# Two layers of a hybrid decoder on one core: how the squares of the norms are summed, and what the first norm's squares wait for

## The chip, the core and the metric

The kernel runs on one core of a Trainium2 chip. The metric is the device time of one execution in microseconds (us), as the median of several runs. Engines are named as the profile names them: PE (matrix multiply; PEld is its weight load), DVE (vector engine), ACT (scalar engine), POOL (GpSimd), SP (the queue that issues every DMA of this kernel).

## The reference, cut to what matters

The input is one sequence of 256 tokens with 1024 channels, in float32, and two layers are applied to it. Each layer does this:

```python
xn = rms(x, norm_mix_g)          # x * rsqrt(mean(x*x) + 1e-6) * g
z  = xn @ w_in                   # 7756 columns: mLSTM, sparse attention, differential attention, gates
...                              # three mixers give y_a, y_b, y_c, 512 channels each
x  = x + (sum_b sigmoid(gate_b) * (y_b @ w_branch[b])) @ w_out
xn = rms(x, norm_ffn_g)
g, u = split(xn @ w_gate_up)     # 2 x 2816 columns
x  = x + (silu(g) * u) @ w_down
```

So there are four RMS norms in all: each needs, for every token, the sum of the squares of its 1024 channels.

## The kernel before, in words

**Data.** x is held transposed in SBUF: eight tiles `x[0]` to `x[7]` of 128 channels by 256 tokens (T = 256). The weights come from HBM in chunks of 128 x 1024 floats (512 KB, `chunk`, line 509): a DMA into `raw` (3 buffers), then `split` (line 524): ACT copies it to `whi` in a rounded 32-bit format and DVE subtracts to get the rest, `wlo` (3 buffers each). Each product is three matmuls (`feat`, line 528): whi times the high part of x, whi times its low part, wlo times the high part. The high and low parts of x times the norm's gain are `xg` (`fx` in the norm before the feed-forward), made by `gained` (line 547).

**The norm** (`norm`, line 551) doesn't scale x before the matmuls. It makes the gained parts, and beside them the factor of each token, which is multiplied in when results leave PSUM. The factor: the squares of the eight x tiles are summed into one tile `nacc` of 128 x 256. Two PE transposes bring it to token-major form in PSUM, a DVE reduce over 128 columns gives the sum for each token (`rcol`), DVE and POOL make the reciprocal root, DVE spreads it (`rc`), four PE transposes bring it back, and ACT copies it to `rB`. In the first norm of the program (`first`) two ACT instructions of 1024 columns make the squares (`sq8`) and three DVE additions of 1024, 512 and 256 columns fold them. In the other three norms ACT squares `x[0]` straight into `nacc`, squares the others one by one into `nsq`, and POOL adds each of these seven to `nacc`.

**The opening.** x comes in four DMAs and the first two chunks in halves; `first_pair` (line 630) multiplies them in the order in which they land. The squares of the first norm are recorded with `S.after(w_first[1][1])`: they come after all writes to the low part of the second chunk. The chunks from the third on go through `chunk` in the loop over the pairs of output blocks (`fp`, line 778). Results of a pair leave PSUM through `pad`, a DVE multiplication by `rB`, and a chain of DVE operations (`cv`) follows.

**The order of work.** Nothing is issued as it is written. Each call is recorded with an index; `S.early(n)` lowers the index by n. `schedule` (line 206) then simulates the five engines with a duration for each operation (`cost`, line 354): on each engine it takes the recorded operation that could start first, by index among equals, and holds operations until a buffer of their tag is free. The engines run the resulting lists strictly in order. `S.gang()` makes the matmuls inside it one uninterrupted block. Temporary tiles of tag `w` share 15 buffers (`tmp`, line 473). `PLACED` (line 416) lists the tags whose tiles are laid out first in SBUF, with gaps in bytes.

Of the kernel before, what the change touches and what calls it, by code (L numbers as in the profile page):

```python
# [11 lines left out]
F32 = mybir.dt.float32  # L12
F32R = mybir.dt.float32r
BF16 = mybir.dt.bfloat16
AF = mybir.ActivationFunctionType
OP = mybir.AluOpType
AX = mybir.AxisListType.X
# [376 lines left out]
T = 256  # L394
# [18 lines left out]
BR = (1, 2, 0)  # L413


PLACED = ("whi", "wlo", "nacc", 192, "xg", "y", "h", 192, "w", 224, "mqk", 192, "K1", 416)


def plan():
# [37 lines left out]
def kernel(ctx: ExitStack, tc: tile.TileContext, xT: bass.AP, wts: bass.AP, cst: bass.AP,  # L457
# [6 lines left out]
    S = Order(tc, sbuf, psum)  # L464
    V, A, G, PE, SP = (S.engine(n) for n in ("vector", "scalar", "gpsimd", "tensor", "sync"))
# [4 lines left out]
    def atps(shape):  # L470
        return S.tile(shape, F32, tag="at", name="at", bufs=4, psum=True)

    def tmp(shape, name="w"):
        return S.tile(shape, F32, tag="w", name=name, bufs=NW)
# [6 lines left out]
    K1 = S.tile([128, 256], F32, name="K1")  # L481
# [3 lines left out]
    xs = S.tile([128, 128 + 8 * T], F32, name="x")  # L485
    x = [xs[:, 8 + k * T:8 + (k + 1) * T] for k in range(8)]
    ident, ones = K1[:, 0:128], K1[:, 128:256]
# [19 lines left out]
    widx = [0]  # L507

    def chunk(li):
        i = widx[0]  # L510
        widx[0] += 1
        w = WIDTH[i]
        raw = S.tile([128, CH], F32, tag="raw", name="raw", bufs=3)
        hi = S.tile([128, CH], F32R, tag="whi", name="whi", bufs=3)
        lo = S.tile([128, CH], F32R, tag="wlo", name="wlo", bufs=3)
        src = wts[li, OFFS[i]:OFFS[i + 1]].rearrange("(p c) -> p c", p=128)
        with S.early(600):
            if li == 0 and i < 2:
                return raw, hi, lo, src
            SP.dma_start(raw[:, :w], src)  # L520
            split(raw, hi, lo, 0, w)
        return hi, lo
# [28 lines left out]
    def norm(gcol, wide, xg=None):  # L551

        first = xg is not None
        xg = xg or []
        acc = S.tile([128, T], F32, tag="nacc", name="nacc")
        for k in range(8 - len(xg)):
            g = gcol[:, k:k + 1]
            if not wide:
                a = S.tile([128, 2, T], F32R, tag="xg", name="xg", bufs=8)
            else:  # L560
                if k % 4 == 0:
                    y4 = S.tile([128, 4, 2, T], F32R, tag="y", name="fx", bufs=3)
                a = y4[:, k % 4]
            gained(a, k, g)
            xg.append(a)
        if first:
            sq = S.tile([128, 8 * T], F32, tag="y", name="sq8", bufs=3)
            with S.after(w_first[1][1]):
                for a in (0, 4 * T):
                    A.activation(sq[:, a:a + 4 * T], xs[:, 8 + a:8 + a + 4 * T], AF.Square)  # L570
            for n in (4 * T, 2 * T):
                V.tensor_add(sq[:, 0:n], sq[:, 0:n], sq[:, n:2 * n])
            V.tensor_add(acc, sq[:, 0:T], sq[:, T:2 * T])
        else:
            for k in range(8):
                if k == 0:
                    A.activation(acc, x[k], AF.Square)
                else:
                    sq = tmp([128, T], "nsq")
                    A.activation(sq, x[k], AF.Square)  # L580
                    G.tensor_add(acc, acc, sq)
        ps = atps([128, 2, 128])
        with S.gang():
            for t in range(2):
                PE.transpose(ps[:, t, :], acc[:, t * 128:(t + 1) * 128], ident)
        rcol = S.tile([128, 2], F32, tag="rcol", name="rcol", bufs=2)
        V.tensor_reduce(rcol, ps, axis=AX, op=OP.add)
        V.tensor_scalar(rcol, rcol, 1.0 / D, EPS, op0=OP.mult, op1=OP.add)
        rsqrt_cols(rcol, 2)
        rr = tmp([128, 2, 128], "rc")  # L590
        V.tensor_copy(rr, rcol[:, :, None].to_broadcast([128, 2, 128]))
        ps = atps([128, 2, T])
        with S.gang():
            for i in range(2):
                for t in range(2):
                    PE.transpose(ps[:, i, t * 128:(t + 1) * 128], rr[:, t, :], ident)
        rB = S.tile([128, T], F32, tag="rB", name="rB", bufs=2)
        A.activation(rB, ps[:, 0, :], AF.Copy)
        return xg, rcol, rB


    xg0, w_first = [], [chunk(0), chunk(0)]
    with S.early(10 ** 6):
# [21 lines left out]
        w_first = [w[1:3] for w in w_first]  # L625
# [4 lines left out]
    def first_pair(ps):  # L630
        with S.early(10 ** 6), S.chained():
            keep_warm(WARM)
            seen = [0, 0]

            def passes(j, ks):

                for p, q in ((0, 0), (0, 1), (1, 0)):
                    for k in ks:
                        seen[j] += 1
                        PE.matmul(ps[:, j, :], w_first[j][p][:, k * 128:k * 128 + 128], xg0[k][:, q, :],  # L640
                                  start=sum(seen) == 1, stop=sum(seen) == 48)

            for j, ks in ((0, (0, 1)), (0, (2, 3)), (1, (0, 1, 2, 3)), (0, (4, 5)), (1, (4, 5)),
                          (0, (6,)), (1, (6,)), (0, (7,)), (1, (7,))):
                passes(j, ks)
# [113 lines left out]
                                       op0=OP.mult, op1=OP.subtract)  # L759

    for li in range(L):
        widx[0] = 2 if li == 0 else 0
        c = col[li]
        r = row[li] = S.tile([128, R_N], F32, tag="row", name="row")
        ps_first = mmps([128, 2, T]) if li == 0 else None
        if li == 0:
            first_pair(ps_first)
        xg, rcol, rB = norm(c[:, C_NM:C_NM + 8], False, xg0 if li == 0 else None)
        if li:
            SP.dma_start(r, rows[li:li + 1, :].to_broadcast([128, R_N]))  # L770
# [6 lines left out]
        mqk = []  # L777
        for fp in range(4):
            if li == 0 and fp == 0:
                ps = ps_first  # L780
            else:
                ps = mmps([128, 2, T])
                for j in range(2):
                    w = chunk(li)
                    for k in range(8):
                        feat(ps[:, j, :], w, k * 128, xg[k], k == 0, k == 7)
            qk = S.tile([128, 2, T], F32, tag="mqk", name="mqk", bufs=4)
            for j in range(2):
                f = 2 * fp + j
                pad = pads[j]  # L790
                with S.early(400):
                    V.tensor_mul(pad[:, 3:3 + T], ps[:, j, :], rB)
                v = tmp([128, T], "cv")
                cw = c[:, C_CW + 4 * f:C_CW + 4 * f + 4]
                A.activation(v, pad[:, 0:T], AF.Identity, scale=cw[:, 0:1], bias=c[:, C_CB + f:C_CB + f + 1])
                for m in range(1, 4):
                    V.scalar_tensor_tensor(v, pad[:, m:m + T], cw[:, m:m + 1], v, op0=OP.mult, op1=OP.add)
                A.activation(qk[:, j, :], v, AF.Silu)
            mqk.append(qk)
            if li == 0 and fp == 2:  # L800
                with S.after(w[1]):
                    SP.dma_start(K2, cst[:, 256:1024])
                    SP.dma_start(col[1], cols[1])
            if li == 0 and fp == 3:
                with S.after(w[1]):
                    SP.dma_start(r, rows[li:li + 1, :].to_broadcast([128, R_N]))
                hb, dg, rope = setup(li)


        ps = [mmps([128, 256]) for _ in range(2)]  # L810
        for a in range(2):
            w = chunk(li)
            for t in range(2):
                for kk in range(4):
                    k = 4 * a + kk
# [6 lines left out]
        for t in range(2):  # L822
            j = tmp([128, 256], "junk")
# [19 lines left out]
        for ks in ((0, 1, 2), (3, 4, 5), (6, 7)):  # L843
            w = chunk(li)
# [28 lines left out]
        for t in range(2):  # L873
            nk = 128 * (t + 1)
            m = mask1[:, 128:256] if t == 0 else mask1
            acc = tmp([128, 256], "isc")[:, :nk]
            ps = [atps([128, 2, nk]) for _ in range(2)]
# [5 lines left out]
            for j in range(2):  # L883
                p = ps[j]
                rl = tmp([128, 2, nk], "rl")
                A.activation(rl, p, AF.Relu)
                for hp in range(2):
                    h = 2 * hp + j
# [23 lines left out]
        p = proj512()  # L912
# [5 lines left out]
        w = chunk(li)  # L918
        p = [mmps([128, 512]) for _ in range(2)]
# [4 lines left out]
        w = chunk(li)  # L924
        sv = []
        for t in range(2):
            p = mmps([128, 512])
# [5 lines left out]
        y = [S.tile([128, 4, 2, T], F32R, tag="y", name=f"y{b}", bufs=3) for b in range(3)]  # L933
        for t in range(2):
            yp = atps([128, 4, 128])
            n = 4 // (t + 1)
            for a in range(t + 1):
# [13 lines left out]
                with S.gang():  # L951
                    for i in range(n):
                        for kt in range(t + 1):
                            for j in range(2):
                                h = 2 * n * a + 2 * i + j
# [5 lines left out]
        p = tmp([128, 2, 64], "lamp")  # L961
# [11 lines left out]
        for j, dst in ((2, dqT), (3, dkT)):  # L973
            p = proj512()
# [4 lines left out]
        p = proj512()  # L979
        dv = [evac(p[t], rcol[:, t:t + 1]) for t in range(2)]  # L980
        for t in range(2):
            n = 4 // (t + 1)
# [4 lines left out]
            for hh in range(0, 4, n):  # L987
# [9 lines left out]
                a = tmp([128, nh, nk], "da")  # L997
# [4 lines left out]
                with S.gang():  # L1002
                    for i in range(nh):
                        h = hh + i
# [4 lines left out]
            j = tmp([128, 4, 128], "dj")  # L1009
# [34 lines left out]
        with S.gang():  # L1044
            for t in range(2):
                p = atps([128, 4, 128])
# [21 lines left out]
        for t in range(2):  # L1068
            p = mB[t]
# [11 lines left out]
        for b, (si, ti) in enumerate(((0, 0), (1, 1), (0, 1))):  # L1081
            p = atps([128, 4, 128])
# [7 lines left out]
        p = proj512()  # L1090
# [7 lines left out]
        p = proj512()  # L1098
        mo = [evac(p[t], rh[:, t:t + 1], AF.Tanh).rearrange("p (h d) -> p h d", h=4) for t in range(2)]
        for t in range(2):  # L1100
# [9 lines left out]
            for a in range(2):  # L1110
                V.tensor_copy(den[:, 2 * a:2 * a + 2], nd[a][:, :, 128])
                for i in range(2):
                    j = tmp([128, 128], "mj")
# [25 lines left out]
        for gp in range(12):  # L1139
            ps = mmps([128, 2, T])  # L1140
            for j in range(2):
                w = chunk(li)
# [13 lines left out]
        for n, b in enumerate(BR):  # L1156
            for ep in range(4):
                w = chunk(li)
# [125 lines left out]
```

## Time and profile before

| | |
|---|---|
| median of 3 runs | 909.11 us |
| the three runs | 909.11, 903.57, 916.03 us |
| the profiled execution | 910.13 us |
| its span, first to last instruction | 908.0 us |
| granted PE clock over the span | 1.00 |
| busy: PE, PEld, DVE, ACT, POOL | 897.8, 857.3, 675.6, 536.0, 111.6 us |
| HBM read | 158.27 MB, 175 GB/s over the span |

A line of the timeline gives the start from the beginning of the span, the duration, the engine, the operation with out<-in tiles and shapes, the count, and in brackets the idle time of the engine before it with what ended it. A line of the chain of waits gives start, duration, and the engine and tile that the program's end depended on then. Nearly all instructions carry line 323, from which the planner issues them, so work is told apart by tiles. 2.1 us of the profiled execution lie outside the span.

### The profile page before, as it was taken

The page shows a single profiled execution, that of the slowest core. Times are in us where ns is not written, and L with a number is a line of the kernel's source. Part 1 is how long each engine was busy: PE and PEld are TensorE (multiplying, and loading weights), DVE is VectorE, ACT ScalarE, POOL GpSimd, SP SyncE. Part 2 cuts the span into 40 slices and gives each one's busy share as a digit, 9 for nine tenths or more (in the row PEclk, how much of TensorE's full clock was granted, in tenths as well). Part 3 has the DMA queues.
Part 4 walks back from the last instruction along what each step waited for, and adds up shares of the span by engine and source line. Part 5 has one row for each costly group of instructions (what it writes and reads, how often), then busy time and mean ns, then how long its engine had stood idle before and what let it go on. Part 6 is the DMA issues. An engine that isn't in the chain of part 4 may idle for free.

```text
span 908.0 us, 18059 instructions
## 1 busy us (share of the span) xinstructions
PE 897.8 (99%) x7162; PEld 857.3 (94%) x7162; DVE 675.6 (74%) x1276; ACT 536.0 (59%) x928; POOL 111.6 (12%) x142
## 2 busy tenths in 40 slices
PE   9999999999999999999999999999999999999998
PEld 8978779999999999999999787899999999999998
DVE  6999989766896666665578899897669866666553
ACT  6786677765465444444457857687654655545442
POOL 0333342300021000000110221312000300000000
PEclk9999999999999999999999999999999999999999
DMA  8665524356555555555665554433555555555663
GB/s 260 197 200 183 165 91 126 123 176 196 196 187 186 187 186 187 186 176 189 190 188 181 181 186 141 138 110 125 186 190 194 198 185 191 197 195 189 197 210 102
DMA packets 46453, 160.50 MB, mean 177 GB/s; under 512 B 5408, under 2 KB 6560, under 8 KB 46368
## 3 DMA queue, kind: packets, MB, share of 16 engines
q1 hardware_dynamic: 46368, 159.34, 53.8%
q8 instruction: 56, 0.92, 0.4%
q14 instruction: 29, 0.24, 0.1%
HBM read 158.27 MB, written 1.05 MB: 175 GB/s over the span
## 4 chain that ended last, share of the span: by engine, by line
PE 88%; DVE 6%; POOL 2%; DMA 2%; issue 1%; ACT 1%; ACTq 0%; DVEq 0%
PE mm L323 83%; PE at L323 5%; DVE e L323 2%; DVE wlo L323 2%; POOL s L323 2%; DMA raw<-in_wts_dram 1%; ACT whi L323 1%; DMA x<-in_xT_dram 0%; DVE zr L323 0%; DVE cv L323 0%; DVE y L323 0%; DVE s L323 0%; DVE rot L323 0%; DVE pad L323 0%; DVE xg L323 0%
## 5 line engine op out<-in xcount | busy, mean ns | idle before, releaser
L323 ACT ACTIVATE whi<-raw 128x1024 fp32r<-128x1024 f32 (+3 forms) x304 | 316.5, 1042 | 316.6 <-PE mm L323 150.3
L323 DVE TENSOR_TENSOR wlo<-raw,whi 128x1024 fp32r<-128x1024 f32 (+3 forms) x304 | 364.5, 1200 | 170.8 <-ACT whi L323 169.0
L323 PE MATMUL mm<-fx,whi 128*128 128x256 f32 x1408 | 245.1, 279 | 0.0
L323 PEld LDWEIGHTS mm<-fx,whi 128*128 128x128 f32 x1408 | 214.7, 189 | 0.0
L323 PE MATMUL mm<-fx,wlo 128*128 128x256 f32 x704 | 195.9, 279 | 0.0
L323 PE MATMUL mm<-xg,whi 128*128 128x256 f32 x1024 | 181.4, 280 | 0.3 <-ACT whi L323 0.3
L323 PEld LDWEIGHTS mm<-xg,whi 128*128 128x128 f32 x1024 | 155.4, 188 | 1.7 <-issue 0.7
L323 PE MATMUL mm<-whi,xg 128*128 128x512 f32 (+2 forms) x512 | 149.1, 372 | 1.1 <-DVE pad L323 1.1
L323 PE MATMUL mm<-xg,wlo 128*128 128x256 f32 x512 | 142.5, 281 | 0.8 <-DVE wlo L323 0.8
L323 PEld LDWEIGHTS mm<-fx,wlo 128*128 128x128 f32 x704 | 132.0, 188 | 0.0
L323 PE MATMUL mm<-h,whi 128*128 128x256 f32 x704 | 122.1, 279 | 0.0
L323 PEld LDWEIGHTS mm<-whi,xg 128*128 128x128 f32 x512 | 92.0, 188 | 17.3 <-issue 1.5
L323 PEld LDWEIGHTS mm<-h,whi 128*128 128x128 f32 x704 | 107.4, 189 | 0.0
L323 PE MATMUL mm<-h,wlo 128*128 128x256 f32 x352 | 98.1, 279 | 0.0
L323 PEld LDWEIGHTS mm<-xg,wlo 128*128 128x128 f32 x512 | 95.8, 188 | 1.1 <-DVE wlo L323 1.1
L323 PE MATMUL mm<-wlo,xg 128*128 128x512 f32 (+2 forms) x256 | 94.9, 371 | 0.0
L323 PEld LDWEIGHTS mm<-h,wlo 128*128 128x128 f32 x352 | 66.1, 188 | 0.0
L323 PE MATMUL mm<-y,whi 128*128 128x256 f32 x384 | 65.4, 276 | 0.0
L323 POOL TENSOR_TENSOR nacc<-nacc,nsq 128x256 f32<-128x256 f32 x21 | 20.2, 962 | 348.0 <-ACT nsq L323 210.1
L323 PEld LDWEIGHTS mm<-y,whi 128*128 128x128 f32 x384 | 57.8, 188 | 0.0
L323 PEld LDWEIGHTS mm<-wlo,xg 128*128 128x128 f32 x256 | 48.1, 188 | 7.3
L323 PE MATMUL mm<-y,wlo 128*128 128x256 f32 x192 | 53.0, 276 | 0.0
(199 smaller groups left out, 1083.6 us busy)
## 6 DMA issues: line engine op xcount, KB each, us to landing
raw<-in_wts_dram SPq DMA_DIRECT2D x278, 512.0 KB, 3.4
raw<-in_wts_dram SPq DMA_DIRECT2D x16, 384.0 KB, 3.8
raw<-in_wts_dram SPq DMA_DIRECT2D x4, 498.0 KB, 4.0
raw<-in_wts_dram SPq DMA_DIRECT2D x4, 256.0 KB, 4.8
out_dram<-x SPq DMA_DIRECT2D x8, 128.0 KB, 3.4
row<-in_rows_dram SPq DMA_DIRECT2D x2, 388.0 KB, 5.3
x<-in_xT_dram SPq DMA_DIRECT2D x3, 256.0 KB, 5.0
raw<-in_wts_dram SPq DMA_DIRECT2D x2, 332.0 KB, 3.0
```

The source lines that it names most:

```text
L323: getattr(getattr(nc, o.eng), o.fn)(*args, **kw)
```

## The change

- In `norm`, the accumulator becomes a temporary of tag `w` with two parts of 256 columns, and `nacc` is no longer a tile of its own (1 KB in each partition, taken out of `PLACED`).
- In the three later norms the square of `x[7]` goes from ACT into the second part; POOL adds six squares, not seven. Four transposes instead of two, and the reduce goes over 256 columns for each token.
- In the first norm the two halves of the squares wait for the high parts of the third and the fourth chunk, one each. DVE folds them with two additions (1024 and 512 columns); the last fold is left to the reduce.
- The calls of `chunk` for the third and fourth chunk are recorded right after `first_pair`, before the norm, and used in the loop.

```diff
-PLACED = ("whi", "wlo", "nacc", 192, "xg", "y", "h", 192, "w", 224, "mqk", 192, "K1", 416)
+PLACED = ("whi", "wlo", 192, "xg", "y", "h", 192, "w", 224, "mqk", 192, "K1", 416)
...
-        acc = S.tile([128, T], F32, tag="nacc", name="nacc")
+        acc = tmp([128, 2, T], "nacc")
...
-            with S.after(w_first[1][1]):
-                for a in (0, 4 * T):
-                    A.activation(sq[:, a:a + 4 * T], xs[:, 8 + a:8 + a + 4 * T], AF.Square)
-            for n in (4 * T, 2 * T):
-                V.tensor_add(sq[:, 0:n], sq[:, 0:n], sq[:, n:2 * n])
-            V.tensor_add(acc, sq[:, 0:T], sq[:, T:2 * T])
+            for a in range(2):
+                with S.after(w_next[a][0]):
+                    A.activation(sq[:, 4 * a * T:4 * (a + 1) * T], xs[:, 8 + 4 * a * T:8 + 4 * (a + 1) * T], AF.Square)
+            V.tensor_add(sq[:, 0:4 * T], sq[:, 0:4 * T], sq[:, 4 * T:8 * T])
+            V.tensor_add(acc.rearrange("p a t -> p (a t)"), sq[:, 0:2 * T], sq[:, 2 * T:4 * T])
         else:
             for k in range(8):
-                if k == 0:
-                    A.activation(acc, x[k], AF.Square)
+                if k in (0, 7):
+                    A.activation(acc[:, k // 7, :], x[k], AF.Square)
                 else:
                     sq = tmp([128, T], "nsq")
                     A.activation(sq, x[k], AF.Square)
-                    G.tensor_add(acc, acc, sq)
-        ps = atps([128, 2, 128])
+                    G.tensor_add(acc[:, 0, :], acc[:, 0, :], sq)
+        ps = atps([128, 2, 2, 128])
         with S.gang():
-            for t in range(2):
-                PE.transpose(ps[:, t, :], acc[:, t * 128:(t + 1) * 128], ident)
+            for i in range(2):
+                for t in range(2):
+                    PE.transpose(ps[:, t, i, :], acc[:, i, t * 128:(t + 1) * 128], ident)
...
-        V.tensor_reduce(rcol, ps, axis=AX, op=OP.add)
+        V.tensor_reduce(rcol, ps.rearrange("p t a c -> p t (a c)"), axis=AX, op=OP.add)
...
         if li == 0:
             first_pair(ps_first)
+            w_next = [chunk(0), chunk(0)]
...
-                    w = chunk(li)
+                    w = w_next[j] if li == 0 and fp == 1 else chunk(li)
```

## Rows read from the trace of the kernel before

**Rows 1.** The page: span and busy time (share of the span) with instructions.

```profile
span 908.0 us, 18059 instructions
...
PE 897.8 (99%) x7162; PEld 857.3 (94%) x7162; DVE 675.6 (74%) x1276; ACT 536.0 (59%) x928; POOL 111.6 (12%) x142
```

**Rows 2.** Waits of PE, whole span: for whom, us in total, times, longest.

```profile
PE at L323 <- DVE zr L323: 2.0, 2, 1.8
PE mm L323 <- DVE pad L323: 1.1, 1, 1.1
...
PE mm L323 <- DVE wlo L323: 0.8, 1, 0.8
```

**Rows 3.** Windows, PE alone: length, busy us (instructions), granted clock, DMA.

```profile
280.00:460.00 180.00, 180.00 (x1531) 1.00 0.57 185
740.00:880.00 140.00, 140.00 (x1238) 1.00 0.60 196
```

**Rows 4.** Timeline of the opening: ACT.

```profile
10.32 1.05 ACT L323 ACTIVATE sq<-x 128x1024 f32<-128x1024 f32 x1
...
11.27 1.05 ACT L323 ACTIVATE whi<-raw 128x1024 fp32r<-128x1024 f32 x1
...
13.51 1.06 ACT L323 ACTIVATE whi<-raw 128x1024 fp32r<-128x1024 f32 x1 [0.24 <-DMA raw<-in_wts_dram]
...
15.10 1.07 ACT L323 ACTIVATE whi<-raw 128x1024 fp32r<-128x1024 f32 x1 [0.53 <-DMA raw<-in_wts_dram]
```

**Rows 5.** Timeline of the opening: DVE, and PE where it waited.

```profile
13.50 1.22 DVE L323 TENSOR_TENSOR sq<-sq 128x1024 f32<-128x1024 f32 x1
...
13.63 0.39 PE L323 MATMUL mm<-xg,wlo 128*128 128x256 f32 x1 [0.76 <-DVE wlo L323]
...
14.63 1.22 DVE L323 TENSOR_TENSOR wlo<-raw,whi 128x1024 fp32r<-128x1024 f32 x1
...
16.20 1.23 DVE L323 TENSOR_TENSOR wlo<-raw,whi 128x1024 fp32r<-128x1024 f32 x1 [0.35 <-ACT whi L323]
...
17.35 0.68 DVE L323 TENSOR_TENSOR sq<-sq 128x512 f32<-128x512 f32 x1
...
18.07 0.42 DVE L323 TENSOR_TENSOR nacc<-sq 128x256 f32<-128x256 f32 x1
```

**Rows 6.** Chain of waits, 8 to 37 us: start, us, what.

```profile
17.46 5.81 DMA raw<-in_wts_dram
...
23.37 1.07 ACT whi L323
...
34.79 0.34 DVE pad L323
...
35.18 1.91 PE mm L323 x14
```

**Rows 7.** Tile nacc: ns min/median/max, starts; last, who waited for it (us, times).

```profile
L323 POOL TENSOR_TENSOR nacc<-nacc,nsq x21: 742/876/1573, 263.3 to 725.6; 128x256 f32<-128x256 f32 x21
...
L323 PE MATMUL at<-K,nacc x8: 270/272/329, 18.6 to 726.8; 128*128 128x128 f32 x8
...
  PEld at L323: 0.4, 2
```

**Rows 8.** Timeline of the first layer's second norm: ACT, POOL, PE.

```profile
275.68 0.41 ACT L323 ACTIVATE nsq<-x 128x256 f32<-128x256 f32 x1
...
276.23 1.01 POOL L323 TENSOR_TENSOR nacc<-nacc,nsq 128x256 f32<-128x256 f32 x1 [1.72 <-ACT nsq L323]
...
277.30 0.44 PE L323 MATMUL at<-K,nacc 128*128 128x128 f32 x2
```

**Rows 9.** Chain of waits, third norm: the four transposes back.

```profile
468.63 0.44 PE at L323 x4
```

**Rows 10.** DVE reduces: timeline (norm's), groups by shape (512 columns).

```profile
277.77 0.42 DVE L323 TENSOR_REDUCE rcol<-at 128x2 f32<-128x256 f32 x1 [0.25 <-PE at L323]
...
L323 DVE TENSOR_REDUCE s<-sq 128x8 f32<-128x512 f32 x16 | 10.8, 674 | 0.0
```

More of the change, by code (lines that the diff above doesn't have):

```diff
@@ L761 @@
     for li in range(L):
-        widx[0] = 2 if li == 0 else 0
+        if li:
+            widx[0] = 0
         c = col[li]
```

## The prediction

> **What bounds the kernel now.** I read the page first: PE is busy for 897.8 us of a span of 908.0 us [rows 1]. So 10.2 us is all the PE time that could be won by removing waits, and any PE instruction added costs its full issue time unless it falls into one of those waits. The list of PE's waits names the longest: 2.0 us for the tile zr in the attention part, 1.1 us for pad, 0.8 us for wlo [rows 2]. The last two lie in the opening, which the change touches.
>
> The windows come next, because "busy" hides a second thing. In the feed-forward of the first layer 1531 PE instructions take 180 us, 117.6 ns each; in that of the second layer, the same matmuls with the same shapes, 1238 take 140 us, 113.1 ns each [rows 3]. The granted clock is 1.00, which is the 2.4 GHz level, in both. So PE has two paces 4.5 ns apart, and a whole stretch has one or the other. The feed-forward of a layer has 22 x 2 x 24 + 8 x 66 = 1584 matmuls; 1584 x 4.5 ns = 7.1 us. This is far more than any single wait. The slow stretch follows the norm at 277 us, whose transposes and wait are what this change edits. The three runs of the kernel, 903.57, 909.11 and 916.03 us, lie 5.5 and 6.9 us apart, each near this one term; I read them, without proof, as none, one and two feed-forwards at the slow pace.
>
> **The change part by part.**
>
> *Four transposes instead of two*, in each of four norms: 8 more PE instructions. Four transposes on the chain take 0.44 us [rows 9], 0.11 us each; 8 x 0.11 = +0.88 us. Nothing covers this: PE is the bound around the three later norms. In the opening it can fall into a wait, which would leave 6 x 0.11 = 0.66 us.
>
> The page "TensorE: Matmul & The Clock Gate" of the Trainium skill (Part 1, on the 2.5 ns) says that warm matmuls of 128 columns start 55.6 ns apart; by it the eight would cost an estimated 0.44 us and the whole sum would be 0.44 us lower. The trace shows twice that for these float32 transposes [rows 9], and the row decides.
>
> *One POOL addition less in three norms.* An addition takes 0.876 us at the median [rows 7]. In the second norm the last square is done at 275.68 + 0.41 = 276.09 us, the addition ends at 277.24 us, and the transposes start at 277.30 us [rows 8]. With the change they could start about 1.1 us sooner. What PE gets of this is only what its queue waited: 0.4 us, in two places [rows 7]. So -0.4 us; the remaining 0.7 us of each addition lay beside matmuls that PE had in front. If the planner sets the transposes earlier by as much as it thinks the tile is early, the same wait comes back, so the bounds are -0.4 and 0. After that nothing is late: the factor is used only when the first results of the feed-forward leave PSUM, and PE's waits name none of those tiles [rows 2].
>
> *The longer reduce.* 512 columns instead of 256: 0.674 us against 0.42 us [rows 10], so 0.25 us more on DVE four times. In the later norms it lies inside the 1.1 us that the missing addition frees, so I cost it at nothing; without that cover it would delay the factor by 0.25 us, still ahead of its use.
>
> *The first norm's squares.* Now the squares' first half stands at 10.32 us on ACT, the high part of the third chunk right behind it at 11.27 us [rows 4]; its low part comes late and PE waits 0.76 us for it until 13.63 us [rows 5]. After the change that high part starts about 0.95 us sooner, and this wait goes. But PE then waits again: the low part of the fourth chunk is ready only at 14.63 + 1.22 = 15.85 us [rows 5], since its high part starts when its DMA has landed, at 13.51 us [rows 4], which the change doesn't move. And what is gained is not kept: at 35.18 us PE waits 1.1 us for pad [rows 2, 6], and the chain that ends there doesn't pass through the first wait. It goes back over DVE and the high part at 23.37 us to a 5.81 us DMA issued at 17.46 us [rows 6], when the low part of the fifth chunk, 16.20 + 1.23 = 17.43 us [rows 5], freed its raw buffer. PE being early at 13.63 us only makes the wait at 35.18 us longer: 0 us.
>
> What moves that chain is a new order on ACT and DVE. The squares' second half now follows the fourth chunk's high part: 13.51 + 1.06 + 1.05 = 15.62 us, where the fifth chunk's high part starts at 15.10 us today [rows 4]. Behind the squares on ACT stands that high part, and behind it DVE's low part and the DMA of SP's queue that waits for it. The first fold takes 1.22 us on DVE [rows 5]; it can start at 15.85 us, ends at 17.07 us, and the low part then at 18.30 us: 0.87 us later than now. If the low part goes ahead of the fold, only ACT's delay counts, 15.62 - 15.10 = 0.5 us. If both folds go ahead, 0.68 us more [rows 5]: 1.55 us. I take +0.87 us, because now too the squares and the first fold stand directly behind their inputs and ahead of the next chunk's parts on both engines [rows 4, 5]. The third fold that goes, 0.42 us [rows 5], lies where DVE is ahead of the chain: nothing. Bounds: +1.55 us, and -0.76 us if the earlier release of the third chunk's buffer speeds the later DMAs enough to move pad as well.
>
> *Recording the two chunks earlier* moves two DMAs, two ACT copies and two DVE subtractions in the planner's index. Their issue is bound by the three raw buffers, and they already stand ahead of the norm by 600; SP's order of those DMAs should not change: 0 us. If it did, a DMA late by one fold is in the bounds above.
>
> *The tile from tag w and the shifted layout.* One of 15 buffers for a short time: no row shows a wait for one, so 0 us. All later tiles lie 1 KB lower; no row shows a duration that depends on an address, so it is bounded by the two paces: 7.1 us either way, taken as 0.
>
> **Sum.** +0.88 - 0.4 + 0.87 = +1.35 us. The profiled execution, 908.0 us of span and 2.1 us around it, goes from 910.13 to 911.5 us. It lies 1.0 us above the median of the three runs, so for the median I say 909.11 + 1.35 = 910.5 us: no change that can be measured.
>
> **The rivals.**
>
> *The quick pace in the first feed-forward too.* For: PE enters it right after the edited transposes, and one of the three runs already is at 903.57 us. Against: no row shows what sets the pace. 910.5 - 7.1 = 903.4 us. Chance 0.2.
>
> *The slow pace in the second feed-forward too*, slower than before. The place is the fourth norm, at 727 us: twice the transposes, and if PE leaves them at the slow pace and doesn't come back, 1584 matmuls cost 4.5 ns more each: 917.6 us. It decides from the first matmuls behind the four transposes back. For: the run at 916.03 us. Against: the profiled execution passed the same place and was quick at 740 us [rows 3]. Chance 0.2.
>
> *The opening keeps its gain*: -0.76 instead of +0.87 us, 908.9 us. For it speaks that the third chunk's raw buffer is released about 0.9 us earlier; against it, that the chain to 35.18 us runs over the fifth chunk [rows 6]. Chance 0.1.
>
> *The change does not do what it says*: ACT runs in order, and if the planner already had the chunk's copies ahead of the squares, the new waits would be inert, with a sum of +0.48 us, 909.6 us. The squares at 10.32 us ahead of the copy at 11.27 us [rows 4] speak against it. Chance 0.05.
>
> **How the numbers follow.** The forecast has 0.42, the four rivals 0.55, and 0.03 is for a list that the planner upsets elsewhere. The forecast with its bounds alone runs from 909 to 912.5 us. The range has to take in both paces to leave out less than 2 in 10: 903.4 less the opening's gain gives 902, and 917.6 with a little for the upper bound gives 918. About 2%, 18.2 us, is what a measurement of this kernel can tell from no change. Faster by that would need all of PE's 10.2 us of idle time and the 7.1 us, and still more: 0.01. Slower by that would need 18.2 us / 4.5 ns = 4040 more matmuls at the slow pace, or many new waits: 0.02. Within: 0.97.
>
> **What would show it.** In the changed profile: 18 POOL additions on nacc and 16 transposes; no wait of PE for wlo near 13.6 us but one near 15.5 us; the wait for pad near 35 us longer than 1.1 us, ending near 36 us; the queue's wait for nacc gone; the windows 280 to 460 and 740 to 880 us with 117.6 or 113.1 ns for each instruction. The forecast is wrong if the opening's pad wait ends earlier than 35 us, if PE shows new waits at the norms of over 1 us, or if both feed-forwards have the same pace, which moves the time by more than all the rest.

## The result and the profile after

The changed kernel takes 902.81 us at the median of 21 runs (902.22 to 903.54). The kernel before, run beside it, takes 909.65 us (902.23 to 916.91, 21 runs). The ratio is 0.9943, with a 95% interval of 0.9926 to 0.996; it leaves out the runs of before that lie more than 1.5% above its fastest, and the two medians alone give 0.9925. So the change makes the kernel 0.57% faster, well under the 2% that count as a clear verdict. Forecast were 910.5 us, 1.35 us more than before and too little to measure. The time lies in the range from 902 to 918 us, but the median went down by 6.84 us instead of up.

The runs of before fall into three groups: 6 at 902.2 to 903.6, 9 at 908.8 to 910.7 and 6 at 915.2 to 916.9 us. Those of after have the first group only. The change did not move the quick runs; it took the other groups away.

The page of the changed kernel, as [rows 1]:

```profile
span 900.8 us, 18068 instructions
...
PE 890.9 (99%) x7170; PEld 851.2 (94%) x7170; DVE 674.8 (75%) x1275; ACT 536.1 (60%) x928; POOL 109.7 (12%) x139
```

PE is busy 6.9 us less and has 8 instructions more. Its idle time went from 10.2 to 9.9 us, so the gain is not in the waits. The windows over the two feed-forwards, as [rows 3], show where it is:

```profile
280.00:460.00 180.00, 180.00 (x1590) 1.00 0.62 193
740.00:880.00 140.00, 140.00 (x1238) 1.00 0.62 198
```

The second line has the count of before. The first has more instructions in the same 180 us, 113.2 ns each instead of 117.6 (its last 5.5 us now lie behind the feed-forward). The granted clock is 1.00, the 2.4 GHz level, in both kernels. Cut at the same matmuls of both traces (starts of the last matmul of a stage; us), the whole difference is:

```
                                     before   after   difference
to the end of layer 1's w_out        274.07  274.06     -0.01
feed-forward of layer 1              187.32  180.45     -6.87
mixers of layer 2                    207.75  207.59     -0.16
branches and w_out of layer 2         54.29   54.29      0.00
feed-forward of layer 2              180.54  180.43     -0.11
```

So in these two executions 6.87 of 7.15 us come from one feed-forward that changed from the slow to the quick pace. All else that the change adds and removes comes to -0.28 us.

**The opening** changed as described, and kept nothing. ACT, DVE and PE, as [rows 4, 5]:

```profile
10.62 1.06 ACT L323 ACTIVATE whi<-raw 128x1024 fp32r<-128x1024 f32 x1 [0.40 <-DMA raw<-in_wts_dram]
11.59 1.04 ACT L323 ACTIVATE sq<-x 128x1024 f32<-128x1024 f32 x1
13.23 1.06 ACT L323 ACTIVATE whi<-raw 128x1024 fp32r<-128x1024 f32 x1 [0.60 <-DMA raw<-in_wts_dram]
14.19 1.05 ACT L323 ACTIVATE sq<-x 128x1024 f32<-128x1024 f32 x1
15.14 1.04 ACT L323 ACTIVATE whi<-raw 128x1024 fp32r<-128x1024 f32 x1
...
13.00 0.38 PE L323 MATMUL mm<-xg,wlo 128*128 128x256 f32 x1 [0.28 <-DVE wlo L323]
...
15.46 1.22 DVE L323 TENSOR_TENSOR sq<-sq 128x1024 f32<-128x1024 f32 x1
16.60 1.22 DVE L323 TENSOR_TENSOR wlo<-raw,whi 128x1024 fp32r<-128x1024 f32 x1
17.73 0.69 DVE L323 TENSOR_TENSOR nacc<-sq 128x512 f32<-128x512 f32 x1
```

The squares now follow the third and the fourth chunk's copy, and the first fold stands ahead of the fifth chunk's low part on DVE. That part starts at 16.60 us instead of 16.20 us. PE's wait for wlo shrank from 0.76 to 0.28 us, and there is none near 15.5 us. Then the chain of waits, as [rows 6]:

```profile
17.84 5.43 DMA raw<-in_wts_dram
...
23.38 1.07 ACT whi L323
...
34.80 0.35 DVE pad L323
...
35.19 1.92 PE mm L323 x14
```

The DMA is issued 0.38 us later and takes 0.38 us less, so it lands at the same time, and PE goes on at 35.19 us, where it was 35.18 us. Why it lands no later was not followed up. PE's list of waits, as [rows 2], shows an exchange in front of that point; before, its wait for rc was 0.4 us and that for pad 1.1 us:

```profile
PE at L323 <- DVE zr L323: 2.0, 2, 1.8
...
PE at L323 <- DVE rc L323: 0.9, 1, 0.9
...
PE mm L323 <- ACT whi L323: 0.6, 1, 0.6
PE mm L323 <- DVE pad L323: 0.4, 1, 0.4
PE mm L323 <- DVE wlo L323: 0.3, 1, 0.3
```

The wait for rc, the spread factor of the first norm, ends in front of its four transposes at 23.25 us. Behind them the changed kernel's matmuls start 118 ns apart up to the wait for pad, where those of before started 113 ns apart. So the slower of the two paces occurs in the opening too; it costs nothing there, because PE waits for pad afterwards.

**The norms.** The tile nacc as [rows 7], and the second norm on PE as [rows 8]:

```profile
L323 POOL TENSOR_TENSOR nacc<-nacc,nsq x18: 737/863/1579, 263.3 to 716.2; 128x256 f32<-128x256 f32 x18
...
L323 PE MATMUL at<-K,nacc x16: 270/272/273, 18.6 to 719.0; 128*128 128x128 f32 x16
```

```profile
276.21 0.28 PE L323 MATMUL mm<-fx,whi 128*128 128x256 f32 x1
276.33 0.60 PE L323 MATMUL at<-K,nacc 128*128 128x128 f32 x4
276.68 0.36 PE L323 MATMUL mm<-fx,whi 128*128 128x256 f32 x1
```

18 additions and 16 transposes, 1.0 us sooner than before; and in the answer for the tile nobody of PE waits for nacc any more. Before, its weight load waited at the second norm:

```profile
277.29 0.20 PEld L323 LDWEIGHTS at<-K,nacc 128*128 128x128 f32 x2 [0.18 <-POOL nacc L323]
```

The times from the start of one matmul to the start of the next, called spacing from here on, show the pace at each place. Behind a group of transposes one spacing is about 200 ns and the next one to four are mostly 115 to 123 ns, whatever comes after. In the changed kernel the spacing is back at 113 ns by the sixth one at the latest, behind both groups of each later norm. In the kernel before it stayed at 118 ns behind the two transposes of 277.30 us and behind the four of 281 us, through the whole feed-forward, until 469 us.

### The profile page after: what moved, and what is told of

The parts are those of the page before. It is cut to its first block, busy times and chain, and to the rows that moved or that the text cites. A ratio compares the mean times of both kernels' runs of the same rounds, so it can differ in the third digit from the quotient of the medians.

```text
span 900.8 us, 18068 instructions
## 1 busy us (share of the span) xinstructions
PE 890.9 (99%) x7170; PEld 851.2 (94%) x7170; DVE 674.8 (75%) x1275; ACT 536.1 (60%) x928; POOL 109.7 (12%) x139
## 4 chain that ended last, share of the span: by engine, by line
PE 88%; DVE 7%; POOL 2%; DMA 2%; issue 1%; ACT 1%; ACTq 0%; DVEq 0%
PE mm L323 83%; PE at L323 5%; DVE e L323 2%; DVE wlo L323 2%; POOL s L323 2%; DMA raw<-in_wts_dram 1%; ACT whi L323 1%; DMA x<-in_xT_dram 0%; DVE zr L323 0%; DVE cv L323 0%; DVE y L323 0%; DVE s L323 0%; DVE rot L323 0%; DVE pad L323 0%; DVE sq L323 0%
## 5 line engine op out<-in xcount | busy, mean ns | idle before, releaser
L323 PE MATMUL mm<-fx,whi 128*128 128x256 f32 x1408 | 240.3, 276 | 0.0
L323 PEld LDWEIGHTS mm<-fx,whi 128*128 128x128 f32 x1408 | 212.2, 188 | 0.0
L323 PE MATMUL mm<-h,whi 128*128 128x256 f32 x704 | 119.8, 276 | 0.0
L323 POOL TENSOR_TENSOR nacc<-nacc,nsq 128x256 f32<-128x256 f32 x18 | 17.2, 957 | 332.0 <-ACT nsq L323 198.6
```

Source lines behind the costliest of these rows:

```text
L323: getattr(getattr(nc, o.eng), o.fn)(*args, **kw)
```

## Experiments

Two theories of what sets the pace stood at first. **Wait theory**: when PE had to wait in front of a norm's transposes, the pace that follows is left to chance; without a wait it is the quick one. **Count theory**: two transposes leave it to chance, four bring PE back. Rivals were the 1 KB shift of the layout and the opening. Each kernel was run beside the kernel before on the same chip. "Slow feed-forwards" are read from the three groups of times, which lie 6 to 7 us apart, two feed-forwards for each run; in all twelve profiled executions the group of the time and the number of slow feed-forwards in the trace agree.

**e1, the opening's part alone.**

```diff
+            for a in range(2):
+                with S.after(w_next[a][0]):
...
             first_pair(ps_first)
+            w_next = [chunk(0), chunk(0)]
...
```

> The opening's part of the change alone: the squares wait for the third and fourth chunk; one accumulator, seven POOL additions, two transposes and the tile nacc stay. Wait theory (a feed-forward takes one of two paces by chance when PE has waited for the sum of squares in front of the norm's transposes, and always the quick one when it has not): the waits stay, so the times fall into the groups near 903, 910 and 917 us again, the median near 909.7. Count theory (four transposes leave PE at the quick pace, two leave it to chance): the same, 909.7. Layout theory (the 1 KB shift sets the pace): the same, 909.7. Opening theory (what the opening gains is kept, or sets the pace of all that follows): 903, in every run.

Measured: 910.57 us at the median of 8 runs, 2 near 903.5 and 6 from 909.7 to 912.7; before beside it 902.76 us, 21 of 25 runs under 903.4 and 4 near 909.3. The opening doesn't bring the gain. Its 6 slow feed-forwards of 16 are even more than the 4 of 50 beside it (with equal odds, so large a difference comes in about 1 case of 100); why was not followed up. The kernel before shows that its odds are not fixed: here few of its runs are slow.

**e2, the later norms' part alone, old layout, old opening.**

```diff
-PLACED = ("whi", "wlo", 192, ...
+PLACED = ("whi", "wlo", 1024, 192, ...
...
+            with S.after(w_first[1][1]):
+                for a in (0, 4 * T):
...
```

> The later norms' part alone (eighth square beside the sum, four transposes), the opening's squares back at their old place, and a gap of 1 KB in the layout where nacc was, so that all later tiles lie where they lay before. Wait theory and count theory: every run within 1 us of 903, both feed-forwards at 113 ns for each instruction. Layout theory and opening theory: groups near 903, 910 and 917, median near 909.7.

Measured: 11 of 11 runs from 901.6 to 903.51, median 902.5: 0 of 22 feed-forwards slow, against 6 of 16 in e1 on the same chip. So the later norms' part keeps them quick without the opening's part and without the new layout. The kernel before has only 4 of 50 here, and 0 of 22 can't be told from that.

**e3, four transposes behind a POOL addition.**

```diff
+                    if k < 7:
+                        G.tensor_add(acc[:, 0, :], acc[:, 0, :], sq)
+                    else:
+                        G.tensor_add(acc[:, 1, :], zero, sq)
```

> The changed kernel, but the eighth square goes into the second part by way of POOL (zero plus square, the same addition of 256 columns), so that the four transposes follow a POOL addition of 0.9 to 1.0 us, as the two did before. Wait theory: PE waits again for nacc at the second and fourth norm, some 0.2 us each, and the times fall into groups near 903, 910 and 917; median near 910. Count theory: every run near 903.

Measured: 903.92 us, 11 of 11 runs from 903.09 to 905.56. It looks like a vote for the count, but the expected wait was not there: PE's weight load waited for nacc 0.2 us in one place only, in the opening. Inconclusive, and e6 repeats it with a wait.

**e4, two transposes, later.**

```diff
     if op.eng == "gpsimd":
+        if n == 256 and op.fn == "tensor_add":
+            return 1.2
```

> The kernel before, with two transposes and seven POOL additions; only the planner is told that an addition of 256 columns on POOL takes 1.2 us, so that it puts the transposes behind more matmuls and PE should not wait for nacc. Wait theory: every run near 902 to 903, both feed-forwards at 113 ns, without any part of the change. Count theory: groups near 903, 910 and 917, median near 909.7.

Measured: 917.82 us, 6 runs, 2 near 911 and 4 near 918: 10 of 12 feed-forwards slow. As first put, the wait theory falls. But the wait had moved (timeline of PE at the second and fourth norm):

```profile
278.13 0.38 PE L323 MATMUL at<-K,nacc 128*128 128x128 f32 x2
281.42 0.66 PE L323 MATMUL at<-K,rc 128*128 128x128 f32 x4 [0.20 <-DVE rc L323]
...
721.16 0.38 PE L323 MATMUL at<-K,nacc 128*128 128x128 f32 x2
724.47 0.66 PE L323 MATMUL at<-K,rc 128*128 128x128 f32 x4 [0.30 <-DVE rc L323]
```

With nacc later, rc was late for its four transposes. So the wait theory was widened to both groups, and three kernels were to set each case by itself.

**e5, e4 with the transposes of rc later too.**

```diff
...
         if op.kw.get("op") == OP.pow:
-            return 0.3 + n * 0.165
+            return 1.9 if n == 2 else 0.3 + n * 0.165
```

> As e4 (two transposes, seven POOL additions, the planner told 1.2 us for an addition of 256 columns), and the planner is also told 1.9 us for the reciprocal root of two columns, so that the four transposes of rc come later too; in e4 PE no longer waited for nacc but for rc, 0.3 to 0.4 us at the second and fourth norm. Wait theory, widened (a feed-forward's pace is left to chance when PE waited at either group of transposes in front of it, and is the quick one when it waited at neither): every run within 1.5 us of 903, with two transposes. Count theory (two transposes leave it to chance, four do not): groups near 903, 910 and 917, as in e4.

Measured: 903.43 us, 11 of 12 runs from 902.89 to 904.17, one at 909.91: 1 of 24 feed-forwards slow. Against e4's 10 of 12 that is few: with two transposes too, the feed-forwards are mostly quick when PE doesn't wait for rc. But before beside it has 6 of 58, so e5 is not shown to be better than the kernel before. Its windows from 300 to 440 and 750 to 880 us (PE busy and instructions, clock, DMA):

```profile
300.00:440.00 140.00, 140.00 (x1238) 1.00 0.57 193
750.00:880.00 130.00, 130.00 (x1149) 1.00 0.60 197
```

Both are 113 ns for each instruction. The quick pace is 1238 and 1149 instructions in these windows, the slow one 1191 and 1106.

e5 doesn't set the two transposes of nacc free of waits, either. PE's weight load waited for DVE's part of the gained x (`fx`, at the third norm `xg`), three or six matmuls ahead of each of the three groups:

```profile
276.80 0.19 PEld L323 LDWEIGHTS mm<-fx,whi 128*128 128x128 f32 x1 [0.23 <-DVE fx L323]
457.44 0.19 PEld L323 LDWEIGHTS mm<-xg,whi 128*128 128x128 f32 x1 [0.22 <-DVE xg L323]
720.22 0.19 PEld L323 LDWEIGHTS mm<-fx,whi 128*128 128x128 f32 x1 [0.22 <-DVE fx L323]
```

Behind all three groups the spacing is 118 ns, up to the four transposes of rc, and behind those it is 113 ns. In e4 the same waits stand at the same places, so neither kernel has taken away the waits around nacc.

**e6, four transposes with a real wait for nacc.**

```diff
+        if n == 256 and op.fn == "tensor_add":
+            return 0.02
... (and the lines of e3)
```

> As e3 (four transposes, the eighth square by way of POOL), but the planner is told that an addition of 256 columns on POOL takes 0.02 us, so that the transposes come some three matmuls sooner and PE really waits for nacc, about 0.3 us at the second and the fourth norm; in e3 it waited there less than 0.05 us. Wait theory: runs in groups near 904, 911 and 918. Count theory: every run near 904.

Measured: 903.89 us, 12 of 12 runs from 903.37 to 905.51. The wait was there (timeline of PE, second norm):

```profile
276.41 0.38 PE L323 MATMUL at<-K,nacc 128*128 128x128 f32 x2
277.13 0.44 PE L323 MATMUL at<-K,nacc 128*128 128x128 f32 x2 [0.34 <-POOL nacc L323]
```

The wait falls between the second and the third transpose, and the pace is 113 ns behind each of the three groups. The wait theory, as it stood, misses here: it forecast three groups of times. The count theory fits here, and it missed in e5, where it forecast the times of e4.

**e7, the changed kernel with a wait for rc.**

```diff
-            return 0.3 + n * 0.165
+            return 0.02 if n == 2 else 0.3 + n * 0.165
```

> The changed kernel, only the planner is told that the reciprocal root of two columns takes 0.02 us instead of 0.63 us, so that the four transposes of rc come about 0.5 us sooner and PE should wait for rc some 0.2 us at the later norms; nothing waits for nacc. Wait theory: runs in groups near 903, 910 and 917, as the wait is directly in front of the feed-forward. Count theory: every run near 903.

Measured: 12 runs, 1 at 905.43, 4 from 912.97 to 914.86, 7 from 919.23 to 920.24: 18 of 24 feed-forwards slow. The count theory falls: four and four transposes don't help when PE waits at the last group. The wait stands ahead of the first of the four transposes (PE's weight load at the second norm, in the quickest run):

```profile
279.10 0.42 PEld L323 LDWEIGHTS at<-K,rc 128*128 128x128 f32 x4 [0.24 <-DVE rc L323]
```

This quickest run, with both feed-forwards quick, is still 2.6 us above the median of the changed kernel; in the traces 2.2 us of the difference lie between the two feed-forwards.

**e8, e7 with four transposes of a constant in each feed-forward; e7 again; the changed kernel again.**

```diff
             hs.append(h)
+            if f == 1:
+                dm = atps([128, 4, 128])
+                with S.gang(), S.after(h):
+                    for i in range(4):
+                        PE.transpose(dm[:, i, :], ident, ident)
```

> e7 (PE waits for rc, feed-forwards mostly at the slow pace) with one group of four transposes more in each feed-forward, behind the second pair of blocks, of a constant, waiting for nothing, result unused; 0.44 us each, 0.9 us in all. Theory of the last group (a group of four transposes that PE enters without waiting brings it back to the quick pace, whatever was before): most runs near 906 us, which is e7's quickest run plus 0.9 us plus at most 12 us of each feed-forward at the slow pace (0.5 us). Theory of the wait alone (what a wait has set stays until the next norm): groups as in e7 plus 0.9 us, most runs at 914 to 921.

> e7 once more, on the chip of e8, as its measure: groups near 905, 913 and 920 us, most of them above 912, if the odds of the two paces are the kernel's; if they are the chip's, other odds, with the groups at the same places.

> The changed kernel itself, on another chip than at first. By the theory of the last group every run lies near 902.8 whatever the chip, while the kernel before has some runs near 909 and perhaps 916; the ratio of the medians depends on the odds that the kernel before has on this chip: 1.000 where most of its runs are quick, 0.993 where its median run has one slow feed-forward.

Measured: e8 has 3 runs at 906.88 to 907.21, 3 at 913.32 to 913.56 and 1 at 920.43: 5 of 14 feed-forwards slow. e7 again has 0, 3 and 3 runs in its groups: 9 of 12 slow. So a later group can bring PE back, but not always. (5 of 14 against e7's 27 of 36 in both sessions; against the 9 of 12 beside it alone the runs are too few.) The profiled execution of e8 has both outcomes, and that of e7 has two slow ones (windows of e8, then of e7 again):

```profile
300.00:440.00 140.00, 140.00 (x1238) 1.00 0.57 191
750.00:880.00 130.00, 130.00 (x1106) 1.00 0.57 188
```

```profile
300.00:440.00 140.00, 140.00 (x1191) 1.00 0.55 185
750.00:880.00 130.00, 130.00 (x1106) 1.00 0.57 188
```

In e8's first feed-forward the spacing is 118 ns up to the four added transposes at 292.3 us and 113 ns from the third matmul behind them; in its second it is 118 ns on both sides of them. "Whatever was before" in the expectation was too strong: from the slow pace it is a matter of odds.

The changed kernel again: 902.9 us, 11 of 11 runs from 902.39 to 904.03. Before beside it: 902.99 us, 16 of 18 runs under 904.3. The ratio here is 0.9992, interval 0.9974 to 1.001. None of its 22 feed-forwards is slow, where e7, the same kernel with a wait for rc, has 9 of 12 on the same chip. The size of the gain depends on how often the kernel before falls into the slow pace: in 21 of 42 feed-forwards in the first comparison, in 4 of 50 on the chip of e1 to e4, in 8 of 94 on the chip of e5 to e8. On the chip of e8 the gain can't be seen in the median.

**What the twelve profiled executions show together** at the two groups of transposes of the three later norms, 72 groups, and at e8's two added ones. A wait counts as ahead of a group when a spacing of 220 ns or more, instead of 113 to 118, stands at most seven matmuls before its first transpose, whatever PE waited for:

```
group of transposes                                  back to 113 ns within 15 matmuls
four, no wait ahead, quick pace before it              33 of 34
four, no wait ahead, slow pace before it               10 of 13  (two of the 13 are e8's added groups)
four (nacc, e6), a wait between its transposes          3 of 3
four (11 of rc, 1 of nacc), a wait ahead of it          3 of 12
two (nacc), a wait ahead of it                          2 of 12
two (nacc), no wait ahead of it                        in no trace
```

In the changed kernel both groups are of the first kind. In the kernel before the two transposes are of the fifth kind and mostly leave PE slow, and the four of rc then are of the second. The kinds were drawn when the traces were known, so this is a reading and not a test. It fits every kernel above, and e7 against the changed kernel shows one part of it by itself: the same groups of transposes, only with a wait ahead of those of rc, leave most feed-forwards slow. The other part stays open. With a wait ahead, two transposes and four come back about as seldom, and two without a wait ahead never occurred. At nacc the change takes the wait away and doubles the transposes, and no run here tells which of the two it was. What inside PE holds the pace was not tried and stays open, and so does why the odds of the kernel before differ between the comparisons.

## Why the prediction was wrong, point by point

- **The pace** was the step that failed. The prediction had found the two paces, the 7.1 us between them and the place where the slow one starts, and put the change's effect on it at nothing, with the same chance for both directions. The term measured -6.87 us in the profiled pair: the changed kernel enters the feed-forward quick, in 0 of 42 cases slow, where the kernel before had 21 of 42 slow. The rows read then held a hint: the slow stretch began behind the instruction with the wait that the change removes. The rival of the slow side held that twice the transposes could leave PE slow; behind groups of four without a wait ahead it was quick in 43 of 47 cases. The rival of the quick side, 903.4 us at a chance of 0.2, is what happened. That the median moved by it is in part luck of the comparison: on the chip of e8 the ratio is 0.9992, as the forecast of no change would have it.
- **Four transposes, the missing addition and the longer reduce**, +0.88, -0.4 and 0 us. The spacing of the transposes is 0.109 us in the changed trace, and PE's wait for nacc is gone. The reduce takes 0.69 us, as forecast, in front of a factor that is still early. In the second layer's feed-forward, quick in both traces, their net is -0.11 us, where +0.22 - 0.2 = +0.02 us was forecast. Right within 0.13 us, and the rest is the pace again: between the two groups of the fourth norm the kernel before ran 30 matmuls at 118 ns, 0.13 us longer than at 113.
- **The opening**, +0.87 us. Half of it happened: the low part starts 0.40 us later, as ACT's copies came earlier than reckoned (13.23 for 13.51 us). It was not passed on: the DMA behind it landed at the same time. The chain was right, and that a delay at its head is handed on one to one was wrong: the wait for pad was to be longer than 1.1 us and to end near 36 us, and it is 0.4 us and ends at 35.19 us, where it ended before. The wait for wlo near 15.5 us didn't come. That the earlier PE gain at 13.6 us is lost again was right, but in another place: not at pad, but at rc, for which PE waits 0.9 instead of 0.4 us, and by the slow pace behind it. The prediction had said that PE's waits name no tile of the factor; rc, in the opening, is one.
- **Recording the chunks earlier, the tile of tag w, the layout**: nothing, and nothing was found; e2 has the old layout and the same time.
- **The three runs as none, one and two slow feed-forwards**: right by all that is on record, the three groups of the 21 runs and the twelve traces with none, one or two slow feed-forwards in the group of their time.
- **Within 2%**: right. With the pace of the first feed-forward in the sum, the center would have been 903 to 904 us. The upper bound of 912.5 us comes out only from the profiled execution's 910.13 us, with +0.88 and +1.55 us; from the median, 909.11 us, they give 911.5 us.

## What to carry to other kernels

When runs of one kernel fall into groups with fixed distances, look for one stretch whose instructions all take a few per cent longer at the same granted clock, and for the instruction where it begins; a change of that instruction can be worth more than every wait in the list. Here a wait of PE of 0.24 us ahead of four short matmuls was enough to make a stretch of 1584 matmuls 7 us longer in most cases (e7: 27 of 36 feed-forwards). Compare such kernels by the counts in each group and on more than one chip, because a median of few runs measures the odds. And look in the trace whether a kernel that is to have no wait has none: in e5 it had moved by a few matmuls to another tile.

## What was not expected of the hardware

PE ran the same alternation of weight load and 256-column matmul at 113.3 or 117.8 ns from start to start (the two feed-forwards of the kernel before), with a granted clock of 1.00 in both, and kept either pace for over 1500 matmuls. The page "TensorE: Matmul & The Clock Gate" of the Trainium skill (Part 1, on the 2.5 ns) gives N/2.4 GHz plus 2.5 ns for back-to-back matmuls, an estimated 109.2 ns for 256 columns; here, with a weight load for each matmul, the traces show neither pace at that value, and the measurement decides. The pace changed at groups of short matmuls: behind 43 of 47 groups of four transposes without a wait ahead it was the quick one, behind 5 of 24 groups, of two or four, with a wait ahead. The odds of one kernel, the one before, were 21 of 42 slow feed-forwards in one comparison and 4 of 50 and 8 of 94 in others.
